# An S5 and gated DeltaNet step on one core: the second supertile's input projection, taken chunk by chunk

## The chip, the core and the metric

The kernel runs on one core of a Trainium2 chip. TensorE (PE in the profile) multiplies matrices into PSUM, VectorE (DVE) and ScalarE (ACT) do elementwise work, GpSimd (POOL) does more of it, and SyncE (SP) issues DMA transfers, as ACT and POOL can too. Each engine works through its own instructions in an order that is fixed when the program is built, and waits for the others on semaphores. The metric is the device time of one execution in microseconds (us); of several runs the median counts.

## What is computed

A two-layer streaming encoder step over 2048 prompt positions and 8 x 16 sample positions, width 1024. Cut to what matters here:

```python
def trunk(x, c, ...):
    cs = jax.nn.silu(c)
    for i in range(DEPTH):                      # layer 0: S5, layer 1: gated DeltaNet
        mod = cs @ w_ada[i] + b_ada[i]
        shift, scale, gate = jnp.split(mod[:, None, :], 3, axis=-1)
        h = rms_norm(x, norm_g[i]) * (1.0 + scale) + shift
        ...                                     # the mixer of the layer, on h
        x = x + gate * out
    y = rms_norm(x, final_g)

def s5_branch(h, ...):
    proj = h @ w_in
    u, z = jnp.split(proj, 2, axis=-1)
    ...                                         # scan over u, gates, output projection
```

The prompt has one row of `c`, so one shift and one scale per channel; each of the eight sample sequences has its own. The change lies in the first lines of layer 0: the norm and modulation of x and the product that gives `u`.

## The kernel before

**Tiling.** Channels lie on the partitions. The 2176 positions are eight supertiles of 272 columns (`NCH`): 256 of the prompt (`NPC`) and 16 of the samples. A supertile's x is a tile of 128 partitions by 8 chunks of channels by 272 columns. Its u has eight blocks of 128 output channels. Each block is one PSUM tile, the sum over the eight chunks. `mm3` (L146) makes a float32 product of three matmuls per chunk: the high part of the weight times the high part of x, high times low, low times high. "High" is a copy in a narrower type (`hh`), "low" (`hl`) is what is left of x after the high part is taken away.

**Norm and modulation.** `norm_sq` (L249) squares x on ACT and adds halves on DVE, `norm_r` (L259) sums over channels with a matmul into the tile `ms` and takes square root and reciprocal, and `norm_mul` (L270) multiplies all eight chunks by it in one DVE instruction. `apply_mod` (L277) then multiplies by the scale and adds the shift, sample columns on DVE for all chunks together, prompt columns on ACT chunk by chunk, makes high and low parts for halves of four chunks, and stores h to memory (L299). For supertile 1 it is called with `first=True`: ACT writes the high part at once, and DVE does the modulation in place a second time, followed by one subtraction per half for the low part.

**Order.** Engine proxies `T`, `V`, `S`, `SY` (L57) can be put in an ordered mode: then each instruction on them is held behind the one written before it. Outside this mode a planner that runs at build time orders each engine's instructions. Supertile 0 (L380 to L412) is ordered, chunk by chunk, while weights arrive. Its PSUM tiles for blocks 2 to 5 come from a pool of four (`psd4`), the others from a pool of two (`psd`). L413 to L425 is the passage of the change: the norm of supertile 1's x (`xt1`), evictions of blocks 0 and 1 (`first_copy`, L373, an ACT copy and a store), the split of the last two weight blocks, `apply_mod` of supertile 1, and then the products of blocks 6 and 7 of supertile 0 and the evictions of blocks 2 to 7. PE's own order has the norm's matmul first and blocks 6 and 7 of supertile 0 behind it. After that the loop at L567 takes supertiles 1 to 7: for each of eight blocks one PSUM tile from `psd4`, 24 matmuls, an eviction (`store_u`, L307). Ahead of the fifth block of each supertile (cb == 4) it modulates the next one and loads the one after it. For j == 0 it does no products; it takes `hnext`, loads x2 and norms it, ordered behind the passage above on DVE and ACT.

**Work beside it.** Operations on small tables fill DVE: `transitions` (L483) and the chains ahead of it may run at any time, `rot_table` (L552) only behind the last ordered DVE instruction of the passage (`after`, L424). The pools `sq`, `acc` and `r` of the norm have one buffer each; x has three, so that x4's load waits for the store of h from supertile 1. `SY` is ordered until L581.

Of the kernel before, what the change touches and what calls it, by code (L numbers as in the profile page):

```python
# [10 lines left out]
F32 = mybir.dt.float32  # L11
F32R = mybir.dt.float32r
I32 = mybir.dt.int32
AF = mybir.ActivationFunctionType
ALU = mybir.AluOpType
# [3 lines left out]
P = 128  # L19
D = 1024  # L20
KC = 8
NTOK = 2176
NCH = 272
NPC = 256
# [17 lines left out]
def bc(ap, axis, n):  # L42
    a = ap.unsqueeze(axis)
    shape = list(a.shape)
    shape[axis] = n
    return a.broadcast_to(shape)
# [7 lines left out]
def kernel(ctx: ExitStack, tc: tile.TileContext, I, O, upto="Z"):  # L54
    nc = tc.nc
# [18 lines left out]
    T, V, S, G, SY = (Engine(e) for e in (nc.tensor, nc.vector, nc.scalar, nc.gpsimd, nc.sync))  # L74
# [10 lines left out]
    h0_d = [dr.tile([D, NCH], F32, name=f"h0_d{i}") for i in range(8)]  # L85
# [23 lines left out]
    modT = cst.tile([P, 48, 9], F32, name="modT")  # L109
    gs0 = cst.tile([P, 8, 9], F32, name="gs0")  # L110
# [35 lines left out]
    def mm3(ps, w_hi, w_lo, x_hi, x_lo, part=None):  # L146
        n = len(w_hi)
        for k in part or range(n):
            T.matmul(ps, lhsT=w_hi[k], rhs=x_hi[k], start=(k == 0), stop=False)  # L149
            T.matmul(ps, lhsT=w_hi[k], rhs=x_lo[k], start=False, stop=False)  # L150
            i_ = T.matmul(ps, lhsT=w_lo[k], rhs=x_hi[k], start=False, stop=(k == n - 1))  # L151
        return i_.ins
# [51 lines left out]
    def pairs(pool, nm):  # L204

        t = {(o, i): pool.tile([P, KC, P], F32R, tag=f"{i}{o}", name=f"{nm}{i}{o}")
             for o in range(7, -1, -1) for i in "hl"}
        return [t[o, "h"] for o in range(8)], [t[o, "l"] for o in range(8)]
# [4 lines left out]
    def ks(t, n=KC):  # L213
        return [t[:, k] for k in range(n)]
# [4 lines left out]
    wu_hi, wu_lo = pairs(wp, "wu")  # L219
    ev = pab.enter_context(tc.tile_pool(reuse_waits="tile", name="ev", bufs=3))  # L220
    xz = pab.enter_context(tc.tile_pool(reuse_waits="tile", name="xz", bufs=1))
    psd = pab.enter_context(tc.tile_pool(reuse_waits="tile", name="psd", bufs=2, space=PSUM))
# [4 lines left out]
    def split_x(nm, xt, hf):  # L227
        a = hp.tile([P, 4, NCH], F32R, tag="hh", name=f"hh{nm}_{hf}")
        b = hp.tile([P, 4, NCH], F32R, tag="hl", name=f"hl{nm}_{hf}")
        spl["i"] = [S.copy(a, xt).ins, V.tensor_sub(b, xt, a.bitcast(F32)).ins]  # L230
        return ks(a, 4), ks(b, 4)

    with ExitStack() as pa:
# [6 lines left out]
        hp = pa.enter_context(tc.tile_pool(reuse_waits="tile", name="hp", bufs=4))  # L240
        psn = pa.enter_context(tc.tile_pool(reuse_waits="tile", name="psn", bufs=1, space=PSUM))
        psd4 = pa.enter_context(tc.tile_pool(reuse_waits="tile", name="psd4", bufs=4, space=PSUM))

        def load_x(j):
            xt = xp.tile([P, KC, NCH], F32, tag="x", name=f"x{j}")
            ld = SY.dma_start(xt, I["xT"][:, j * NCH:(j + 1) * NCH].rearrange("(k p) n -> p k n", p=P))
            return xt, ld.ins

        def norm_sq(xt, sqs=None):  # L249
            acc = sp1.tile([P, 2, NCH], F32, tag="acc", name="acc")  # L250
            for hf in range(2):
                sq = sqs[:, 4 * hf:4 * hf + 4] if sqs else sp1.tile([P, 4, NCH], F32, tag="sq", name="sq")
                xh = xt[:, 4 * hf:4 * hf + 4]
                S.activation(sq, xh, AF.Square)
                V.tensor_add(sq[:, 0:2], sq[:, 0:2], sq[:, 2:4])
                V.tensor_add(acc[:, hf], sq[:, 0], sq[:, 1])
            return acc

        def norm_r(acc, r=None, fold=False):  # L259
            ps = psn.tile([P, NCH], F32, tag="ms", name="ms")  # L260
            if fold:
                V.tensor_add(acc[:, 0], acc[:, 0], acc[:, 1])
            for hf in range(1 if fold else 2):
                T.matmul(ps, lhsT=onesd, rhs=acc[:, hf], start=(hf == 0), stop=(fold or hf == 1))
            r = sp1.tile([P, NCH], F32, tag="r", name="r") if r is None else r
            S.activation(r, ps, AF.Sqrt, bias=epst)
            V.reciprocal(r, r)
            return r

        def norm_mul(xt, r):  # L270
            V.tensor_mul(xt, xt, bc(r, 1, KC))
            return xt

        def norm_x(xt, fold=False):
            return norm_mul(xt, norm_r(norm_sq(xt), fold=fold))

        def apply_mod(j, xt, first=False):  # L277
            xs = xt[:, :, NPC:NCH].rearrange("p k (q h) -> p k q h", h=2)
            V.tensor_mul(xs, xs, bc(gs0[:, :, 1:9], 3, 2))
            V.tensor_add(xs, xs, bc(modT[:, 0:8, 1:9], 3, 2))  # L280
            hl = []
            for hf in range(2):
                k4 = range(4 * hf, 4 * hf + 4)
                if not first:
                    for k in k4:
                        xk = xt[:, k, 0:NPC]
                        S.activation(xk, xk, AF.Identity, scale=gs0[:, k, 0:1], bias=modT[:, k, 0:1])
                    hl.append(split_x(j, xt[:, 4 * hf:4 * hf + 4], hf))
                    continue
                a, b = (hp.tile([P, 4, NCH], F32R, tag=t, name=f"{t}{j}_{hf}") for t in ("hh", "hl"))  # L290
                S.copy(a[:, :, NPC:NCH], xt[:, 4 * hf:4 * hf + 4, NPC:NCH])
                for i, k in enumerate(k4):
                    xk = xt[:, k, 0:NPC]
                    S.activation(a[:, i, 0:NPC], xk, AF.Identity, scale=gs0[:, k, 0:1], bias=modT[:, k, 0:1])
                    V.tensor_scalar(xk, xk, gs0[:, k, 0:1], modT[:, k, 0:1], op0=ALU.mult, op1=ALU.add)
                V.tensor_sub(b, xt[:, 4 * hf:4 * hf + 4], a.bitcast(F32))
                hl.append((ks(a, 4), ks(b, 4)))
            (h0, l0), (h1, l1) = hl
            nc.scalar.dma_start(h0_d[j].rearrange("(k p) n -> p k n", p=P), xt)  # L299
            return h0 + h1, l0 + l1  # L300
# [6 lines left out]
        def store_u(j, cb, ps):  # L307
            o = eva.tile([P, NCH], F32, tag="o", name=f"ev{j}_{cb}")
            S.copy(o, ps)
            nc.scalar.dma_start(u_d[cb][j], o)  # L310
# [7 lines left out]
        pd0 = [(psd if cb < 2 else psd4).tile([P, NCH], F32, tag="d", name=f"pd0_{cb}") for cb in range(6)]  # L318
        h0 = [[hp.tile([P, 4, NCH], F32R, tag=f"h{i}", name=f"h{i}0_{hf}") for hf in range(2)] for i in "hl"]
        hcur = [ks(t[0], 4) + ks(t[1], 4) for t in h0]  # L320
# [52 lines left out]
        def first_copy(cb):  # L373
            store_u(0, cb, pd0[cb])
# [12 lines left out]
        for k in range(KC):  # L387
# [5 lines left out]
            if k == 6:  # L393
                xt1 = load_x(1)[0]
# [18 lines left out]
        acc1 = norm_sq(xt1, xsq)  # L413
        first_copy(0)
        first_copy(1)
        for w in raws:
            split_raw(*w)
        hnext = apply_mod(1, norm_mul(xt1, norm_r(acc1)), True)
        for cb in range(2, 8):
            if cb > 5:  # L420
                pd0 += [psd.tile([P, NCH], F32, tag="d", name=f"pd0_{cb}")]
                mm3(pd0[cb], ks(wu_hi[cb]), ks(wu_lo[cb]), *hcur)
            first_copy(cb)
        after = [V.last]  # L424
        T.ordered = V.ordered = S.ordered = False  # L425
        nc.scalar.dma_start(h0_d[0].rearrange("(k p) n -> p k n", p=P), xcur)
# [140 lines left out]
        for j in range(8):  # L567
            hh, hl = hcur
            T.ordered = j == 1
            for cb in range(8):  # L570
                if cb == 4:
                    if j < 7:
                        hcur = apply_mod(j + 1, xnext) if j else hnext
                    V.ordered = S.ordered = j == 0
                    if j < 6:
                        xn, xl = load_x(j + 2)
                        if j == 0:
                            xnext = norm_x(xn)
                    V.ordered = S.ordered = False
                    s5_tables(j)  # L580
                    SY.ordered = False  # L581
                    with later(after):
                        for i in range(3 * j, min(3 * j + 3, 16)):
                            rot_table(i)
                if j > 0:
                    ps = psd4.tile([P, NCH], F32, tag="d", name=f"pd{j}_{cb}")
                    i_ = mm3(ps, ks(wu_hi[cb]), ks(wu_lo[cb]), hh, hl)
                    store_u(j, cb, ps)
                if cb == 7 and 0 < j < 6:
                    xnext = norm_x(xn)  # L590
                if j > 1 and cb % 3 == 1:
                    with later([xl, i_]):
                        ada.pop(0)()
# [10 lines left out]
    hp = pab.enter_context(tc.tile_pool(reuse_waits="tile", name="hpz", bufs=3))  # L604
# [214 lines left out]
    with ExitStack() as px:  # L819
# [96 lines left out]
        for j in range(8):  # L916
# [56 lines left out]
            for ob in range(8):  # L973
                if ob > 1:
# [3 lines left out]
                                       op0=ALU.mult, op1=ALU.add)  # L978
# [302 lines left out]
    with pd:  # L1281
# [15 lines left out]
        pd1 = pd.enter_context(ExitStack())  # L1297
# [4 lines left out]
        first = [psd1.tile([P, 512], F32, tag="d", name=f"pc0_{n0}") for n0, n in NATT]  # L1302
# [132 lines left out]
        with ExitStack() as pq:  # L1435
# [51 lines left out]
            for i0, (n0, n) in enumerate(NATT):  # L1487
                ps = psd1.tile([P, 512], F32, tag="d", name=f"pba{n0}")[0:32, 0:n]
                hh, hl = hcols(n0, n)
# [284 lines left out]
    if True:  # L1774
# [159 lines left out]
        for t in range(16):  # L1934
            p, nx = pp[t], pp.get(t + 1)
# [151 lines left out]
```

## Time and profile before

| | |
|---|---|
| runs | 2149.6, 2155.93, 2157.43 us (median 2155.93) |
| profiled execution | 2152.21 us, span 2150.5 us |
| busy share of the span | PE 97%, DVE 73%, ACT 45%, POOL 22% |
| granted TensorE clock, mean | 0.980 |
| PE busy, 0 to 59.2 us | 41.15 us |
| PE busy, 99.2 to 140 us | 40.80 of 40.80 us |

A row of the timeline has the start in us from the span's start, the duration in us, the engine, the line, the operation, the tiles (written <- read) with their shapes, and in brackets the idle time before it and what ended it. Buffer numbers are left out of tile names: `pd` is any PSUM tile of the projection, `hl` the low part of any supertile. Instructions that were issued in ordered mode show L69, the proxy's line, in place of their own. Rows that follow closely on one engine overlap, since the engines are pipelined. In rows of stretches, each engine has its busy us and its count, and behind POOL stand the granted clock (1.00 is full), the busy share of the DMA engines and GB/s.

### The profile page before, as it was taken

How to read it: one execution, taken by the hardware profiler on the slowest of the kernel's cores; microseconds unless marked ns; L12 is line 12 of the kernel's file. 1: busy time of each engine (PE TensorE's matmuls, PEld its weight loads, DVE VectorE, ACT ScalarE, POOL GpSimd, SP SyncE). 2: the span in 40 equal slices, each digit the busy share in tenths (PEclk: the TensorE clock that was granted, in tenths of full speed). 3: DMA queues.
4: the chain of work that ended last, by engine and by line, in shares of the span. 5: the costliest groups of instructions: out<-in, count | busy, mean ns of one | idle time of the engine just before them, and what ended most of it. 6: DMA issues, size and time to landing. Idle time of an engine off the chain costs nothing. (4 is left out here: it accounts for less than half of the span.)

```text
span 2150.5 us, 42173 instructions
## 1 busy us (share of the span) xinstructions
PE 2086.0 (97%) x15729; PEld 1853.2 (86%) x15729; DVE 1560.0 (73%) x4017; ACT 973.0 (45%) x2290; POOL 477.7 (22%) x720
## 2 busy tenths in 40 slices
PE   6899999999799999999999999999999899999998
PEld 4888988888599999999888879889987788888887
DVE  6999598999756544446665669688546888888875
ACT  3543433333255444446665422341224556666663
POOL 1267410000112222222100000100011344444430
PEclk7999999999899999999999999999999899999999
DMA  9796854454284333336466213663456644444532
GB/s 279 269 300 226 247 150 143 139 161 149 92 243 151 107 113 110 108 100 218 139 207 181 83 42 86 161 147 101 137 165 208 201 138 134 133 138 147 147 113 69
DMA packets 395209, 332.40 MB, mean 155 GB/s; under 512 B 88026, under 2 KB 358890, under 8 KB 395004
## 3 DMA queue, kind: packets, MB, share of 16 engines
q1 hardware_dynamic: 259084, 226.56, 35.8%
q10 hardware_dynamic: 133104, 95.49, 13.9%
q0 software_dynamic: 2816, 7.65, 1.0%
q8 instruction: 124, 2.03, 0.4%
q14 instruction: 81, 0.66, 0.1%
HBM read 213.01 MB, written 116.61 MB: 153 GB/s over the span
## 5 line engine op out<-in xcount | busy, mean ns | idle before, releaser
L149 PE MATMUL pc<-h1h,wdh 128*128 128x512 f32 (+1 forms) x600 | 216.4, 361 | 0.0
L150 PE MATMUL pc<-h1l,wdh 128*128 128x384 f32 (+1 forms) x600 | 214.8, 358 | 0.3 <-POOL h1l L1340 0.3
L151 PE MATMUL pc<-h1h,wdl 128*128 128x384 f32 (+1 forms) x600 | 214.9, 358 | 0.0
L1400 DVE SCALAR_TENSOR_TENSOR ac<-pb,convw,ac 128x384 f32<-128x384 f32 (+3 forms) x288 | 163.5, 591 | 3.3
L149 PE MATMUL pdz<-hhz,wzh 128*128 128x272 f32 x512 | 151.3, 296 | 2.0 <-ACT evz L626 2.0
L150 PE MATMUL pdz<-hlz,wzh 128*128 128x272 f32 x512 | 152.0, 297 | 0.0
L149 PE MATMUL po<-gh,woh 128*128 128x272 f32 x512 | 148.8, 291 | 2.2 <-ACT gh L933 2.2
L151 PE MATMUL pdz<-hhz,wzl 128*128 128x272 f32 x512 | 150.7, 294 | 0.0
L149 PE MATMUL pg<-yh,wgh 128*128 128x272 f32 x512 | 148.2, 289 | 1.9 <-ACT evz L626 1.9
L150 PE MATMUL pg<-yl,wgh 128*128 128x272 f32 x512 | 149.1, 291 | 0.0
L151 PE MATMUL po<-gh,wol 128*128 128x272 f32 x512 | 148.6, 291 | 0.0
L151 PE MATMUL pg<-yh,wgl 128*128 128x272 f32 x512 | 148.2, 289 | 0.0
L150 PE MATMUL po<-gl,woh 128*128 128x272 f32 x512 | 147.8, 289 | 0.0
L149 PEld LDWEIGHTS pc<-h1h,wdh 128*128 128x128 f32 x600 | 112.6, 188 | 12.3 <-issue 1.7
L150 PEld LDWEIGHTS pc<-h1l,wdh 128*128 128x128 f32 x600 | 112.7, 188 | 10.7 <-issue 0.8
L151 PEld LDWEIGHTS pc<-h1h,wdl 128*128 128x128 f32 x600 | 112.6, 188 | 10.1 <-issue 0.8
L149 PE MATMUL pd<-hh,wuh 128*128 128x272 f32 x384 | 112.5, 294 | 0.0
L69 PE MATMUL epo<-w2h,ohi 128*128 128x512 f32 x272 | 111.5, 410 | 0.0
L151 PE MATMUL pd<-hh,wul 128*128 128x272 f32 x384 | 110.9, 289 | 0.0
L150 PE MATMUL pd<-hl,wuh 128*128 128x272 f32 x384 | 110.6, 288 | 0.0
L69 PE MATMUL epo<-w2h,olo 128*128 128x512 f32 x272 | 106.9, 393 | 0.0
L69 PE MATMUL epo<-w2l,ohi 128*128 128x512 f32 x272 | 106.9, 393 | 0.0
(613 smaller groups left out, 6335.9 us busy)
## 6 DMA issues: line engine op xcount, KB each, us to landing
wa<-in_w_ada SPq DMA_DIRECT2D x32, 512.0 KB
wdr<-in_w_in SPq DMA_DIRECT2D x24, 512.0 KB
h_d<-x ACTq DMA_DIRECT2D x8, 1088.0 KB
u_d<-ev ACTq DMA_DIRECT2D x64, 136.0 KB
hz<-h_d SPq DMA_DIRECT2D x16, 544.0 KB
u<-u_d SPq DMA_DIRECT2D x16, 544.0 KB
z_d<-evz ACTq DMA_DIRECT2D x64, 136.0 KB
y_d<-y ACTq DMA_DIRECT2D x32, 272.0 KB
```

The lines of the kernel that those rows point to most:

```text
L69: i_ = f(*a, **kw)
L149: T.matmul(ps, lhsT=w_hi[k], rhs=x_hi[k], start=(k == 0), stop=False)
L150: T.matmul(ps, lhsT=w_hi[k], rhs=x_lo[k], start=False, stop=False)
L151: i_ = T.matmul(ps, lhsT=w_lo[k], rhs=x_hi[k], start=False, stop=(k == n - 1))
L1400: V.scalar_tensor_tensor(o, src(j), convw[:, b, j:j + 1], o, op0=ALU.mult, op1=ALU.add)
```

## The change

Supertile 1's modulation leaves `apply_mod` and is written out in the passage. The sample columns of all chunks are normed and modulated first. The evictions of blocks 2 to 5 of supertile 0 are put ahead of the modulation, which frees the four tiles of `psd4`; these are taken by blocks 0 to 3 of supertile 1 at once. Then, chunk by chunk, the prompt columns are multiplied by the norm factor, ACT writes the high part, DVE modulates in place and subtracts the low part, and PE multiplies this chunk into all four tiles. The evictions of blocks 6 and 7 come after the second and third chunk, the store of h after the last. In the loop, the first four blocks of supertile 1 have only their evictions left.

```diff
-        def apply_mod(j, xt, first=False):
+        def apply_mod(j, xt):
             xs = xt[:, :, NPC:NCH].rearrange("p k (q h) -> p k q h", h=2)
             V.tensor_mul(xs, xs, bc(gs0[:, :, 1:9], 3, 2))
             V.tensor_add(xs, xs, bc(modT[:, 0:8, 1:9], 3, 2))
             hl = []
             for hf in range(2):
-                k4 = range(4 * hf, 4 * hf + 4)
-                if not first:
-                    for k in k4:
-                        xk = xt[:, k, 0:NPC]
-                        S.activation(xk, xk, AF.Identity, scale=gs0[:, k, 0:1], bias=modT[:, k, 0:1])
-                    hl.append(split_x(j, xt[:, 4 * hf:4 * hf + 4], hf))
-                    continue
-                a, b = (hp.tile([P, 4, NCH], F32R, tag=t, name=f"{t}{j}_{hf}") for t in ("hh", "hl"))
-                S.copy(a[:, :, NPC:NCH], xt[:, 4 * hf:4 * hf + 4, NPC:NCH])
-                for i, k in enumerate(k4):
+                for k in range(4 * hf, 4 * hf + 4):
                     xk = xt[:, k, 0:NPC]
-                    S.activation(a[:, i, 0:NPC], xk, AF.Identity, scale=gs0[:, k, 0:1], bias=modT[:, k, 0:1])
-                    V.tensor_scalar(xk, xk, gs0[:, k, 0:1], modT[:, k, 0:1], op0=ALU.mult, op1=ALU.add)
-                V.tensor_sub(b, xt[:, 4 * hf:4 * hf + 4], a.bitcast(F32))
-                hl.append((ks(a, 4), ks(b, 4)))
+                    S.activation(xk, xk, AF.Identity, scale=gs0[:, k, 0:1], bias=modT[:, k, 0:1])
+                hl.append(split_x(j, xt[:, 4 * hf:4 * hf + 4], hf))
...
         for w in raws:
             split_raw(*w)
-        hnext = apply_mod(1, norm_mul(xt1, norm_r(acc1)), True)
-        for cb in range(2, 8):
-            if cb > 5:
-                pd0 += [psd.tile([P, NCH], F32, tag="d", name=f"pd0_{cb}")]
-                mm3(pd0[cb], ks(wu_hi[cb]), ks(wu_lo[cb]), *hcur)
+
+        r1 = norm_r(acc1)
+        x1s = xt1[:, :, NPC:NCH]
+        V.tensor_mul(x1s, x1s, bc(r1[:, NPC:NCH], 1, KC))
+        x1q = x1s.rearrange("p k (q h) -> p k q h", h=2)
+        V.tensor_mul(x1q, x1q, bc(gs0[:, :, 1:9], 3, 2))
+        V.tensor_add(x1q, x1q, bc(modT[:, 0:8, 1:9], 3, 2))
+        for cb in (6, 7):
+            pd0 += [psd.tile([P, NCH], F32, tag="d", name=f"pd0_{cb}")]
+            mm3(pd0[cb], ks(wu_hi[cb]), ks(wu_lo[cb]), *hcur)
+        for cb in range(2, 6):
             first_copy(cb)
+        pd1 = [psd4.tile([P, NCH], F32, tag="d", name=f"pd1_{cb}") for cb in range(4)]
+        h1 = [[hp.tile([P, 4, NCH], F32R, tag=f"h{i}", name=f"h{i}1_{hf}") for hf in range(2)] for i in "hl"]
+        hnext = [ks(t[0], 4) + ks(t[1], 4) for t in h1]
+        for hf in range(2):
+            S.copy(h1[0][hf][:, :, NPC:NCH], xt1[:, 4 * hf:4 * hf + 4, NPC:NCH])
+            for k in range(4 * hf, 4 * hf + 4):
+                xk, hk = xt1[:, k, 0:NPC], hnext[0][k]
+                V.tensor_mul(xk, xk, r1[:, 0:NPC])
+                S.activation(hk[:, 0:NPC], xk, AF.Identity, scale=gs0[:, k, 0:1], bias=modT[:, k, 0:1])
+                V.tensor_scalar(xk, xk, gs0[:, k, 0:1], modT[:, k, 0:1], op0=ALU.mult, op1=ALU.add)
+                V.tensor_sub(hnext[1][k], xt1[:, k], hk.bitcast(F32))
+                for cb in range(4):
+                    mm3(pd1[cb], ks(wu_hi[cb]), ks(wu_lo[cb]), *hnext, range(k, k + 1))
+                if k in (1, 2):
+                    first_copy(5 + k)
+        nc.scalar.dma_start(h0_d[1].rearrange("(k p) n -> p k n", p=P), xt1)
         after = [V.last]
         T.ordered = V.ordered = S.ordered = False
...
-                if j > 0:
+                if j == 1 and cb < 4:
+                    store_u(1, cb, pd1[cb])
+                elif j > 0:
                     ps = psd4.tile([P, NCH], F32, tag="d", name=f"pd{j}_{cb}")
                     i_ = mm3(ps, ks(wu_hi[cb]), ks(wu_lo[cb]), hh, hl)
                     store_u(j, cb, ps)
```

## The prediction

> **What bounds the kernel now.** I read the page first, then the stretches around the second supertile, then the timelines of TensorE (PE), VectorE (DVE) and ScalarE (ACT) between 49 and 130 us, then PE's waits. The page says that PE is the engine to watch, so a PE gap is worth its length as long as nothing behind it takes it back.
>
> ```profile
> span 2150.5 us, 42173 instructions
> PE 2086.0 (97%) x15729; PEld 1853.2 (86%) x15729; DVE 1560.0 (73%) x4017; ACT 973.0 (45%) x2290; POOL 477.7 (22%) x720
> ```
>
> The stretches show the gap: busy us and instructions of PE, PEld, DVE, ACT, POOL, then the granted clock.
>
> ```profile
> 66.96:72.23 5.27, 0.00 (x1) 0.00 (x1) 5.17 (x26) 4.66 (x12) 0.00 (x0) 0.73 0.86 314
> 72.23:76.20 3.97, 3.97 (x17) 3.97 (x18) 3.97 (x21) 2.36 (x6) 0.00 (x0) 0.50 0.74 255
> 76.20:87.11 10.91, 10.91 (x86) 10.75 (x84) 10.79 (x83) 4.66 (x7) 0.00 (x0) 1.00 0.95 333
> ...
> 128.69:268.80 140.11, 140.11 (x1088) 126.47 (x1085) 109.64 (x521) 55.31 (x98) 86.72 (x224) 1.00 0.80 256
> ```
>
> PE is empty for 5.27 us, then runs at clock 0.50: 17 matmuls in 3.97 us, 0.23 us each, against 0.127 us each in the next row. The pause costs 5.27 + 17 x 0.10 = 7.0 us; that is the most the change can win here. From 128.69 us PE has no hole for 140 us, and DVE is busy in almost all of the three rows above: it is the second engine to watch.
>
> ```profile
> 72.23 0.59 PE L69 MATMUL pd<-hh,wuh 128*128 128x272 f32 x1 [5.27 <-ACT ev L69]
> ...
> 67.57 0.24 ACT L69 CAST hh<-x 128x64 fp32r<-128x64 f32 x1 [5.29 <-DVE x L69]
> 73.47 1.12 ACT L69 ACTIVATE sq<-x 128x1088 f32<-128x1088 f32 x1
> ...
> 64.22 2.42 DVE L69 TENSOR_TENSOR x<-x,r 128x2176 f32<-128x2176 f32 x1
> 66.86 0.28 DVE L69 TENSOR_TENSOR x<-x,gs 128x128 f32<-128x128 f32 x1
> 73.33 1.29 DVE L69 TENSOR_TENSOR hl<-x,hh 128x1088 fp32r<-128x1088 f32 x1
> ```
>
> PE waits for an eviction that ACT does after the whole modulation of x1, and ACT waits 5.29 us for DVE's product over 2176 columns. The second low part is ready at 73.33 + 1.29 = 74.62.
>
> **The first half of supertile 1.** Its 96 matmuls (four blocks, eight chunks, three each) stay 96. The 2.42 us product becomes three sample operations of 128 columns (0.28 us each, with handover about 0.9 in all: 64.22 to 65.1) and eight products of 256 columns; two low parts of 1088 columns become eight of 272. The evictions of blocks 2 to 5 move ahead of the modulation into ACT's 5.29 us of waiting, so they cost nothing; without that cover they would cost PE what they cost now. A chunk is a strict chain, since the in-place modulation on DVE may only write after ACT has read, and DVE's order is written by hand. Supertile 0 has the same chain:
>
> ```profile
> 49.63 0.43 DVE L69 TENSOR_TENSOR x<-x,r 128x272 f32<-128x272 f32 x1
> ...
> 52.27 0.41 DVE L69 TENSOR_SCALAR x<-x,gs,modT 128x256 f32<-128x256 f32 x1
> ...
> 52.78 0.45 DVE L69 TENSOR_TENSOR hl<-x,hh 128x272 fp32r<-128x272 f32 x1
> 53.14 0.42 DVE L69 COPY mA<-ada 128x256 f32<-128x256 f32 x1
> ...
> 51.63 0.60 ACT L69 ACTIVATE hh<-x,modT,gs 128x256 fp32r<-128x256 f32 x1 [3.16 <-DVE gs L69]
> ```
>
> Product 0.43, handover 0.03 (89.51 to 89.54 in the rows of x2 below), ACT's start to DVE's modulation 0.64 (51.63 to 52.27), to the low part 0.51 (52.78), to the next instruction 0.36 (53.14): a step is 1.97 us. PE needs 12 x 0.127 = 1.52 for it, so PE waits 0.45 a step. Chunk 0: 65.1 + 0.43 + 0.03 + 0.64 + 0.51 + 0.45 = 67.16, against PE free at 66.96: the gap shrinks from 5.27 to 0.2. Chunk 7 is ready at 67.16 + 7 x 1.97 = 80.95, and PE is done at 82.5. Before, the same 96 ended at 87.11, with 0.52 of norm sums among them: **PE leads by 4.1 us** there. A step could be 1.7 (no handover between the ends of instructions) or 2.3 (three more small operations between).
>
> **What is late next.** The norm of x2 is ordered by hand behind the last chunk on ACT and DVE, so its first square, at 73.47 now, starts after ACT's chunk 7: 65.56 + 7 x 1.97 + 0.6 = 79.9, **6.4 us later**. Its chain to PE, now:
>
> ```profile
> 75.06 0.72 DVE L69 TENSOR_TENSOR sq<-sq 128x544 f32<-128x544 f32 x1
> 76.30 0.44 DVE L69 TENSOR_TENSOR acc<-sq 128x272 f32<-128x272 f32 x1
> ...
> 82.49 0.62 PE L264 MATMUL ms<-acc,onesd 128*128 128x272 f32 x2
> ...
> 83.15 0.49 ACT L69 ACTIVATE r<-ms,epst 128x272 f32<-128x272 f32 x1 [1.51 <-PE ms L264]
> ...
> 84.24 1.84 DVE L69 RECIPROCAL r<-r 128x272 f32<-128x272 f32 x1
> ...
> 87.09 2.42 DVE L69 TENSOR_TENSOR x<-x,r 128x2176 f32<-128x2176 f32 x1
> ...
> 89.54 0.60 ACT L287 ACTIVATE x<-x,modT,gs 128x256 f32<-128x256 f32 x1 [1.84 <-DVE x L69]
> 92.15 3.54 ACT L287 ACTIVATE x<-x,modT,gs 128x256 f32<-128x256 f32 x7
> 95.86 1.10 ACT L230 CAST hh<-x 128x1088 fp32r<-128x1088 f32 x1
> ...
> 97.86 1.28 DVE L230 TENSOR_TENSOR hl<-x,hh 128x1088 fp32r<-128x1088 f32 x1
> ...
> 99.21 1.08 PE L69 MATMUL ms<-acc,onesd 128*128 128x272 f32 x4
> 99.93 0.87 PE L149 MATMUL pd<-hh,wuh 128*128 128x272 f32 x4
> ```
>
> x2's first low part ends at 99.14 and PE takes it at 99.93: **0.8 us of slack**, the thinnest of the stage. PE will now be there at 82.5 + 12.82 (87.11 to 99.93) + 0.52 (the norm sums that now fall here) = 95.8. The chain takes 25.7 us (73.47 to 99.14). Its own durations are two squares, two pairs of adds (2 x 2.28), 0.62, 0.49, 1.84, 2.42, eight activations (4.1), 1.10, 1.28: 16.4, and 17.0 with a dozen handovers of 0.05. So the low part comes between 79.9 + 17.0 = 96.9 and 79.9 + 25.7 = 105.6. The other 8.7 us are other work in DVE's and ACT's queues: transition and rotation operations, and the squares of later supertiles. One part of it leaves, 34 transition operations, the first and last of which are
>
> ```profile
> 74.68 0.19 DVE L465 TENSOR_TENSOR sm<-gk 128x32 f32<-128x32 f32 x1
> ...
> 94.17 0.18 DVE L505 TENSOR_TENSOR ni<-sm 128x32 f32<-128x32 f32 x1
> ```
>
> at about 0.11 us of queue each, 3.7 us. They fit into DVE's waits in the chunk steps (eight times some 0.9 us: 1.97 less three slots of about 0.35). I take 25.7 - 3.7 = 22.0 us, near the upper end, because DVE's queue was full all this time and the rotation tables, which may start only behind the last chunk, move along with x2. The low part then ends at 101.9 and PE starts supertile 2 at 102.0, **2.1 us later than now**, after a pause of 6.2 us. That is longer than the pause of 5.27, so the slow clock moves here too: 17 x 0.10 = 1.8. Sum: +2.1 + 1.8 = **+3.9 us**. The gain of the first half is spent.
>
> **Behind it.** Supertile 3 has room: its second low part ends at 125.04 and PE starts it at 128.69.
>
> ```profile
> 123.76 1.28 DVE L230 TENSOR_TENSOR hl<-x,hh 128x1088 fp32r<-128x1088 f32 x1
> ...
> 128.69 0.39 PE L149 MATMUL pd<-hh,wuh 128*128 128x272 f32 x1
> ```
>
> If x3 moved by all of 6.4 it would come at 131.4, before the 12 matmuls of its first half are done at 128.7 + 3.9 + 1.5 = 134.1. The store of h moves behind chunk 7 on ACT's queue, and SP's next load waits for that buffer:
>
> ```profile
> 73.61 0.41 ACTq L299 DMA_DIRECT2D h_d<-x  x1
> ...
> 78.94 0.38 SPq L246 DMA_DIRECT2D x<-in_xT  x1
> 79.44 3.22 SPq L180 DMA_DIRECT2D wa<-in_w_ada  x5
> ...
> 107.52 1.07 PE L186 MATMUL ada<-wa,cs 128*32 128x512 f32 x8
> ```
>
> Store to load is 5.3 us. With the store at some 80.5, x4 is issued at 85.8 and the five weight loads queued behind it end their issue at 89.5 instead of 82.7; the first such product is at 107.52, so I cost this at nothing (if they landed after it: up to 7 us more). Evictions of blocks 0 to 3 now fall together after chunk 7, two squares of x2 among them; block 4 needs the first bank 1.1 us after it is complete, so 0 to 0.5 us.
>
> **The time.** The profiled execution took 2152.21 us around its span of 2150.5; +3.9 gives 2156.1. The runs shown, 2149.6 to 2157.43, have their median 3.7 above it. With the profiled one the four average 2153.8, and I add to that: 2157.7, rounded to 2158.
>
> **Rivals.** *The lead is kept.* If x2's chain shrinks to its own durations plus two or so us, its low part comes at 97 to 98.9 and PE starts supertile 2 1 to 2.9 us earlier than now, with a short pause and no slow clock: 2151 to 2153. For it: 8.7 us of the chain is other work, and the norm sum at 82.49 waited 2.2 us for PE (adds of the second half end near 80.2), which runs earlier now. Against: DVE was busy throughout. Chance 0.23.
>
> *x2 stays behind the rotation tables.* DVE's queue then keeps all 25.7 us, or also takes the 4 us of wide table operations that now come after 97.86 us ahead of the low part. (Three tables are 129 operations; 109 of them stand ahead of 97.86, some 20 of this kind behind, at 0.2 us of queue each.)
>
> ```profile
> 99.53 0.28 DVE L451 TENSOR_TENSOR q<-tw,gk 128x128 f32<-128x128 f32 x1
> ```
>
> Every us behind 99.9 counts in full: +5.8 to +9.8, and 1.8 for the clock: 2161 to 2165. It is slower than before, and decides as soon as the low part is ready after 99.9. For it: the low part stood 0.9 us in DVE's queue after its cast was done (95.86 + 1.10 to 97.86). Against: the norm itself comes before the tables in program order. Chance 0.15.
>
> *The clock falls in the chunk loop.* PE would rest 0.45 us in every 1.97. Here is where the trace shows a fall without one long gap:
>
> ```profile
> 1694.85:1697.57 2.72, 0.44 (x16) 0.36 (x16) 2.27 (x5) 2.66 (x12) 1.23 (x1) 0.99 1.04 280
> 1697.58:1704.90 7.32, 6.53 (x88) 5.63 (x88) 5.90 (x13) 3.21 (x16) 3.42 (x2) 0.54 0.05 8
> ```
>
> PE was idle 84% of 2.7 us there; the chunk loop leaves 23% idle, far from it. If it fell all the same, a chunk takes 12 x 0.23 = 2.76 us, the first half ends at 67.2 + 22.1 = 89.3 and supertile 2 starts at 102.6: +2.7, about 2156.5, and the first rival is dead. The Trainium skill, TensorE: Matmul & The Clock Gate, section "A second HAM failure mode: psum-queue depth-cycling", speaks for this case: short idles between groups of matmuls that cycle through PSUM made the clock swing between half and full. By that rule the change would win nothing in its first half; the rows above don't show it for idles this short. Chance 0.05.
>
> *The change doesn't close its gap* (PE still waits for chunk 0, or steps take over 2.3 us): chunk 7 and x2 come 2 to 3 us later still, about 2161. Chance 0.05. A different static order of later stages, better or worse by 10 us or more, has the last 0.04.
>
> **How the numbers follow.** The forecast has 0.48 and by itself spans +1 to +6, 2155 to 2160. The range takes in the first two rivals and the spread of the runs (some 4 us each way): 2148 to 2167. A measurement tells about 0.5% from no change, 10.8 us, which is more than the 7.0 us at stake: within it 0.89; faster needs a better order elsewhere, 0.04; slower needs the second rival's upper end or a worse order, 0.07.
>
> **What would show it.** Right: no 5.27 us gap at 67; eight groups of 12 matmuls some 2 us apart, each waiting for DVE's low part; x2's first square near 80; a PE pause of several us before supertile 2 near 96, released by DVE's L230, with clock 0.50 behind it. Wrong: steps of 1.5 us or over 2.3, a low part of x2 before 98, a pause elsewhere (an eviction before block 4, a weight load near 107), or stages behind 300 us that differ by more than the shift.

## The result and the profile after

The changed kernel takes 2169.05 us (median of 5 runs, 2166.7 to 2173.48), the kernel before 2155.12 us beside it (5 runs, 2149.6 to 2157.43). The ratio is 1.0073, 95% interval 1.0059 to 1.0087: **slower by 0.7%, some 14 us**, where 2158 was forecast and the range ended at 2167. The pause that the change was aimed at became shorter, and another one, twice as long, appeared 30 us later.

The first two lines of the page of the changed kernel:

```profile
span 2166.4 us, 42187 instructions
PE 2093.2 (97%) x15729; PEld 1855.3 (86%) x15729; DVE 1566.2 (72%) x4031; ACT 973.8 (45%) x2290; POOL 488.4 (23%) x720
```

Stretches of it (columns as before: PE, PEld, DVE, ACT, POOL, granted clock, DMA share, GB/s), from the end of supertile 0's products on:

```profile
66.60:68.86 2.26, 0.00 (x1) 0.01 (x1) 0.02 (x1) 0.75 (x2) 0.00 (x0) 1.00 1.08 389
68.86:84.74 15.88, 13.90 (x94) 12.17 (x94) 15.40 (x75) 6.46 (x13) 2.45 (x6) 1.00 0.34 128
...
98.72:111.04 12.32, 3.22 (x9) 1.75 (x9) 12.32 (x41) 8.97 (x14) 10.39 (x26) 0.65 0.68 252
111.04:115.97 4.93, 4.93 (x22) 4.93 (x23) 4.93 (x19) 1.68 (x4) 2.86 (x4) 0.50 0.58 166
...
140.00:280.00 140.00, 140.00 (x1083) 125.52 (x1083) 102.02 (x477) 56.06 (x99) 80.86 (x186) 1.00 0.76 242
```

Row 1 is what is left of the old pause: 2.26 us instead of 5.27. Row 2 is the chunk loop at full clock. Row 3 is the new pause: of 12.32 us PE is busy 3.22, with norm sums and a few first products, and in row 4 it pays with half the clock for the 22 matmuls behind it. From 140 us PE has no hole again. For 4.50 us of the pause PE stands at a norm sum of x4, which its order has ahead of supertile 2; x2's high part is ready only at 105.78, so this wait decides nothing. Here is who ends the new pause (timeline of PE), and what the ending instruction waited for (timelines of DVE and ACT, changed kernel):

```profile
104.62 1.24 PE L264 MATMUL ms<-acc,onesd 128*128 128x272 f32 x2 [4.50 <-DVE acc L256]
105.84 1.27 PE L149 MATMUL pd<-hh,wuh 128*128 128x272 f32 x4
111.04 0.59 PE L150 MATMUL pd<-hl,wuh 128*128 128x272 f32 x1 [3.93 <-DVE hl L230]
```

```profile
92.84 1.84 DVE L69 RECIPROCAL r<-r 128x272 f32<-128x272 f32 x1
...
95.96 2.51 DVE L69 TENSOR_TENSOR x<-x,r 128x2176 f32<-128x2176 f32 x1
...
102.24 1.84 DVE L267 RECIPROCAL r<-r 128x272 f32<-128x272 f32 x1
...
105.70 2.44 DVE L271 TENSOR_TENSOR x<-x,r 128x2176 f32<-128x2176 f32 x1
108.06 0.47 DVE L697 TENSOR_TENSOR ca<-sp 128x288 f32<-128x288 f32 x1
108.75 0.45 DVE L697 TENSOR_TENSOR ca<-sp 128x288 f32<-128x288 f32 x1
109.61 1.37 DVE L230 TENSOR_TENSOR hl<-x,hh 128x1088 fp32r<-128x1088 f32 x1
...
82.48 1.10 ACT L69 ACTIVATE sq<-x 128x1088 f32<-128x1088 f32 x1
...
104.70 1.08 ACT L230 CAST hh<-x 128x1088 fp32r<-128x1088 f32 x1
```

x2's first square starts at 82.48 (73.47 before), and its low part ends at 110.98 (99.14 before). The chain has not only moved, it is 28.5 us long instead of 25.7. Between x2's product (95.96) and x2's low part (109.61) DVE runs the whole reciprocal and product of x3 (L267, L271) and table work of the next stage (`ca`). x2's high part is ready at 105.78, and the low part still waits 3.8 us in DVE's queue. In the kernel before, x2's low part stands at 97.86, ahead of x3's reciprocal and product, which have almost the same times as now:

```profile
102.03 1.85 DVE L267 RECIPROCAL r<-r 128x272 f32<-128x272 f32 x1
...
105.45 2.42 DVE L271 TENSOR_TENSOR x<-x,r 128x2176 f32<-128x2176 f32 x1
```

Where the 15.9 us between the two spans (2150.5 and 2166.4) arise can be read from the same matmul in both: the first one of the z projection, and the first `sp<-sr` product of the last stage. The first pair of rows is before and after, the second pair likewise.

```profile
268.82 0.37 PE L149 MATMUL pdz<-hhz,wzh 128*128 128x272 f32 x1
```

```profile
281.13 0.37 PE L149 MATMUL pdz<-hhz,wzh 128*128 128x272 f32 x1
```

```profile
1605.75 0.49 PE L1237 MATMUL sp<-sr,xf 128*128 128x128 f32 x2
```

```profile
1617.00 0.49 PE L1250 MATMUL sp<-sr,xf 128*128 128x128 f32 x2
```

12.3 us are lost by the z projection, 11.3 by the last stage. Each is a difference of two single executions; experiment 8 shows how far one kernel's can lie apart. The last stage takes 544.7 us in the one profile and 549.4 in the other, though its instructions stand in the same order; the eighth experiment shows that this part is chance.

### The profile page after: what moved, and what is told of

It reads as the page before. It is cut to its first block, busy times and chain, and to the rows that moved or that the text cites. A ratio compares the mean times of both kernels' runs of the same rounds, so it can differ in the third digit from the quotient of the medians.

```text
span 2166.4 us, 42187 instructions
## 1 busy us (share of the span) xinstructions
PE 2093.2 (97%) x15729; PEld 1855.3 (86%) x15729; DVE 1566.2 (72%) x4031; ACT 973.8 (45%) x2290; POOL 488.4 (23%) x720
```

## The experiments

All are the changed kernel with one thing altered, if nothing else is said. Times are medians; the ratio is to runs of the kernel before on the same chip.

### 1. x2's norm no longer ordered

```diff
-                    V.ordered = S.ordered = j == 0
                     if j < 6:
                         xn, xl = load_x(j + 2)
```

> The changed kernel, with one thing taken back: the norm of x2 is not held behind the last chunk on VectorE and ScalarE, the planner may put it into the waits of the chunk loop. Theory A (x2's norm starts too late, and that is the loss): its first square runs well before 82 us, its low part is ready by 95 to 100 us instead of 111, the pause before supertile 2 shrinks from 12 us to 0 to 3, and the kernel takes 2152 to 2158 us. Theory B (VectorE's queue is full up to 110 us whatever the order): the low part stays at 107 to 111 us and the kernel within 3 us of the changed one, 2166 to 2172.

Measured: 2156.58 us (2155.07 to 2160.71), ratio 1.0019 (1.0008 to 1.0031), against 1.0073: about three quarters of the loss are gone. PE no longer pauses before supertile 2. The squares of x2 now run inside the loop:

```profile
67.36 1.11 ACT L254 ACTIVATE sq<-x 128x1088 f32<-128x1088 f32 x1 [4.54 <-DMA sp<-in_cN]
70.09 1.11 ACT L254 ACTIVATE sq<-x 128x1088 f32<-128x1088 f32 x1 [0.97 <-DVE acc L256]
```

```profile
98.10 1.28 DVE L230 TENSOR_TENSOR hl<-x,hh 128x1088 fp32r<-128x1088 f32 x1
```

The first low part of x2 (second fence, DVE) ends at 99.38, as Theory A expected. In this stage the loop pays for it, and supertile 2 starts at 102.88 instead of 99.93: the clock is 0.50 from 71.36 to 74.78, and the planner put other work between the chunks, on DVE x2's reciprocal ahead of the last low part, which slipped to 88.14 (83.06 in the changed kernel). By 1605 us this profile is level with the kernel before (its last stage begins at 1605.41, there at 1605.75). Theory B falls: DVE's queue is not so full that the order wouldn't matter.

### 2. Stores of the early evictions from GpSimd's queue

```diff
-            nc.scalar.dma_start(u_d[cb][j], o)
+            (E or nc.scalar).dma_start(u_d[cb][j], o)
...
         for cb in range(2, 6):
-            first_copy(cb)
+            first_copy(cb, nc.gpsimd)
```

> The changed kernel, with the stores of the four early evictions (blocks 2 to 5 of supertile 0) issued from GpSimd's queue in place of ScalarE's. In the changed kernel ScalarE stands 5 us between them, behind small table loads, and chunk 0 starts 2.6 us later than forecast. If those store issues are what holds ScalarE: the first chunk's high part starts near 65.5 us in place of 68.2, the loop and x2 come 2.6 us earlier, and the kernel takes 2 to 4 us less than the changed one, 2165 to 2167. Rival: ScalarE waits for something else (VectorE's sample columns), and nothing moves.

Measured: 2165.3 us (2163.44 to 2168.17), ratio 1.0055 (1.0036 to 1.0074). The two intervals overlap, but the trace shows the mechanism. ScalarE in the changed kernel, and then here:

```profile
62.64 5.38 ACTq L299 DMA_DIRECT2D u_d<-ev  x3
68.06 0.24 ACT L69 CAST hh<-x 128x64 fp32r<-128x64 f32 x1 [5.00 <-DMA sp<-in_cN]
68.21 0.60 ACT L69 ACTIVATE hh<-x,modT,gs 128x256 fp32r<-128x256 f32 x1
```

```profile
62.28 1.24 ACT L69 COPY ev<-pd 128x272 f32<-128x272 f32 x4
65.54 0.25 ACT L69 CAST hh<-x 128x64 fp32r<-128x64 f32 x1 [2.02 <-DVE x L69]
65.88 0.60 ACT L69 ACTIVATE hh<-x,modT,gs 128x256 fp32r<-128x256 f32 x1
```

Three store issues take 5.38 us there: ScalarE holds at semaphores ahead of the third and the fourth. By the semaphore events in the trace, each store first waits for the completion semaphore that it will use itself, until the transfer that had it before has landed. For the third that is a load of x issued by SP (landed at 66.06, store issued at 66.13), for the fourth SP's load of small tables (67.28 and 67.68). With the stores elsewhere ScalarE waits for VectorE's sample columns only, and chunk 0 starts 2.3 us earlier (65.88 for 68.21), the low part of x2 2.3 us as well (107.33 for 109.61).

### 3 and 5. x3's norm, or the first tables, held behind x2's low part

```diff
                 if cb == 7 and 0 < j < 6:
-                    xnext = norm_x(xn)
+                    with later(spl["i"] if j == 1 else ()):
+                        xnext = norm_x(xn)
```

> The changed kernel, with the norm of x3 held behind the low part of x2 on VectorE and ScalarE. In the changed kernel x3's reciprocal (1.8 us), product (2.4 us) and its adds stand in VectorE's queue ahead of x2's low part. If they are a part of the loss: the low part comes 4 to 7 us earlier (104 to 107 us), and the kernel takes 2162 to 2165 us. If the planner only fills the place with table operations: no change, 2167 to 2171.

Measured: 2166.88 us (2164.22 to 2167.86), ratio 1.0059 (1.0040 to 1.0078). This is nearer to the second forecast: x2's low part is only 2.2 us earlier, behind table operations. DVE:

```profile
107.46 1.30 DVE L230 TENSOR_TENSOR hl<-x,hh 128x1088 fp32r<-128x1088 f32 x1
```

```diff
+                    if j == 1:
+                        after = spl["i"]
                     with later(after):
-                        for i in range(3 * j, min(3 * j + 3, 16)):
+                        for i in range(0 if j == 1 else 3 * j, min(3 * j + 3, 16) if j else 0):
                             rot_table(i)
```

> The changed kernel, with the first rotation tables held on VectorE behind the low part of x2 (in the changed kernel: behind the last chunk of x1). Theory A2 (x2 starts late, and the table operations in VectorE's queue then stretch its chain from 17 to 28 us): the first square stays at 82.5 us, the low part comes at 101 to 105 us instead of 111, the kernel takes 2158 to 2164 us. Theory A1 (only the late start counts, the table operations just fill holes): the low part stays within 2 us of 111 and the kernel at 2166 to 2171.

Measured: 2168.82 us (2168.6 to 2171.45), ratio 1.0068 (1.0053 to 1.0084). Theory A2 falls as it was put, and Theory A1's numbers come out: taking the tables away alone gains nothing. DVE of the kernel with the tables held:

```profile
103.84 1.85 DVE L267 RECIPROCAL r<-r 128x272 f32<-128x272 f32 x1 [2.82 <-ACT r L266]
105.61 0.76 DVE L699 TENSOR_TENSOR ca<-sp 128x288 f32<-128x288 f32 x2
106.92 0.82 DVE L699 TENSOR_TENSOR ca<-sp 128x288 f32<-128x288 f32 x2
107.66 2.42 DVE L271 TENSOR_TENSOR x<-x,r 128x2176 f32<-128x2176 f32 x1
110.00 2.49 DVE L230 TENSOR_TENSOR hl<-x,hh 128x1088 fp32r<-128x1088 f32 x2
```

DVE even stands idle 2.82 us for x3's square root. x2's high part is there by 105.85, when PE uses it, but the low part stands behind `ca` and x3's product until 110.00: a fixed order doesn't let the ready instruction pass. With x3 held instead, rotation tables and `ca` stood there. Each filled the place that the other left. ScalarE took a part too: without the tables x2's product was ready at 95.67 (98.47 in the changed kernel), but a store held ScalarE until 98.12.

### 9. Both held

The two edits of 3 and 5 together.

> The changed kernel, with both the first tables and the norm of x3 held behind the low part of x2; loop and stores as in the changed kernel. Held alone, neither helped much: the planner put the other one into the place. Theory A3 (x2's chain is stretched by whatever the planner finds for VectorE and ScalarE, so both must go): the first square stays at 82, the low part ends at 101 to 104 us instead of 111, and the kernel takes 2159 to 2163 us. Theory A1 (only the late start counts): low part within 2 us of 111, kernel 2167 to 2171.

Measured: 2160.88 us (2159.42 to 2164.29), ratio 1.0025 (1.0014 to 1.0036). Theory A3 holds by the time; the first low part ends at 104.7, a little behind the expected span. Timelines of DVE and PE:

```profile
92.44 2.43 DVE L69 TENSOR_TENSOR x<-x,r 128x2176 f32<-128x2176 f32 x1
103.43 2.49 DVE L230 TENSOR_TENSOR hl<-x,hh 128x1088 fp32r<-128x1088 f32 x2 [7.63 <-ACT hh L230]
```

```profile
103.45 1.28 PE L149 MATMUL pd<-hh,wuh 128*128 128x272 f32 x4 [5.90 <-ACT hh L230]
```

The chain is 23.0 us now (first square 81.75, first low part to 104.7), and DVE idles at its end: ScalarE is last. It has its own obstacle, the same as in experiment 2:

```profile
97.72 0.33 ACTq L299 DMA_DIRECT2D u_d<-ev  x1
98.09 4.04 ACT L285 ACTIVATE x<-x,modT,gs 128x256 f32<-128x256 f32 x8 [3.14 <-DMA wa<-in_w_ada]
```

The product of x2 is ready at 94.87 and ScalarE begins at 98.09, since a store of u ahead of it (issued at 97.72) was held until a weight load had landed (97.64). That load had used the store's completion semaphore before.

### 4. The early evictions alone

The kernel before, with products 6 and 7 and evictions 2 to 5 ahead of the old `apply_mod`:

```diff
-        hnext = apply_mod(1, norm_mul(xt1, norm_r(acc1)), True)
-        for cb in range(2, 8):
-            if cb > 5:
-                pd0 += [psd.tile([P, NCH], F32, tag="d", name=f"pd0_{cb}")]
-                mm3(pd0[cb], ks(wu_hi[cb]), ks(wu_lo[cb]), *hcur)
-            first_copy(cb)
+        r1 = norm_r(acc1)
+        for cb in (6, 7):
+            pd0 += [psd.tile([P, NCH], F32, tag="d", name=f"pd0_{cb}")]
+            mm3(pd0[cb], ks(wu_hi[cb]), ks(wu_lo[cb]), *hcur)
+        for cb in range(2, 6):
+            first_copy(cb)
+        hnext = apply_mod(1, norm_mul(xt1, r1), True)
+        for cb in (6, 7):
+            first_copy(cb)
```

> The kernel before, with only this part of the change: blocks 6 and 7 of supertile 0 and the evictions of blocks 2 to 5 are put ahead of the modulation of x1; no chunk loop, the norm of x2 as before. If the chunk loop is what moves x2 and so causes the loss, this costs nothing: 2152 to 2158 us, supertile 1 starts within 1 us of 72.2, since its low part is ready only then. Rival: the early evictions with their stores on ScalarE's queue are what hurts: 3 us or more slower than before, with ScalarE held between the stores.

Measured: 2155.82 us (2151.89 to 2159.33), ratio 1.0001 (0.9987 to 1.0015). This part by itself costs and wins nothing; the loss needs the chunk loop. ScalarE, here:

```profile
61.73 5.41 ACTq L310 DMA_DIRECT2D u_d<-ev  x3
67.18 0.24 ACT L69 CAST hh<-x 128x64 fp32r<-128x64 f32 x1 [5.09 <-DVE gk L479]
```

The stores hold ScalarE as long as in the changed kernel, but here the hold is covered: in the kernel before, ScalarE waits for VectorE until 67.57 anyway. With the loop VectorE is ready earlier (ScalarE starts at 65.54 in experiment 2), and the stores are what is left.

### 6. The norm product one chunk ahead

```diff
+        norm_k(0)
...
-                V.tensor_mul(xk, xk, r1[:, 0:NPC])
                 S.activation(hk[:, 0:NPC], xk, AF.Identity, scale=gs0[:, k, 0:1], bias=modT[:, k, 0:1])
+                if k < 7:
+                    norm_k(k + 1)          # V.tensor_mul of chunk k+1 by r1
```

> The changed kernel, with the norm product of chunk k+1 on VectorE moved ahead of the in-place modulation of chunk k, so that ScalarE needn't wait for it. If the step of 1.94 us is the chain product, high part, modulation, low part: VectorE's step falls below PE's 1.52 us, ScalarE's chunk 7 and x2's first square come 5 to 6 us earlier (77 us), and as x2's chain follows the kernel takes 2161 to 2165 us. If the step is set by the load of VectorE and not by the chain: step stays at 1.8 to 1.95, kernel 2167 to 2171.

Measured: 2159.96 us (2154.29 to 2171.59), ratio 1.0023 (1.0006 to 1.0040), a little below the expected span. The first and the last low part of the loop, here and then in the changed kernel:

```profile
68.98 0.43 DVE L69 TENSOR_TENSOR hl<-x,hh 128x272 fp32r<-128x272 f32 x1
...
77.98 0.43 DVE L69 TENSOR_TENSOR hl<-x,hh 128x272 fp32r<-128x272 f32 x1
```

```profile
69.37 0.43 DVE L69 TENSOR_TENSOR hl<-x,hh 128x272 fp32r<-128x272 f32 x1
...
83.06 0.50 DVE L69 TENSOR_TENSOR hl<-x,hh 128x272 fp32r<-128x272 f32 x1
```

Seven steps in 9.0 us, 1.29 each, where the changed kernel needs 1.96. So the step was the chain through two engines, not DVE's load. x2's first square follows at 76.98, 5.5 us earlier, and PE takes the second matmul of supertile 2 at 105.32 in place of 111.04.

### 10 and 7. Loop and stores; loop, stores and both holds

> The changed kernel, with the norm product one chunk ahead and the stores of the early evictions on GpSimd's queue, and nothing held behind x2. If the gains add: x2's first square near 74.5 us, its low part ends 2 to 3 us before the 105.3 us that the norm product ahead alone gave, PE starts supertile 2 at 101 to 103.5, and the kernel takes 2155 to 2159 us, so that holding the tables and x3 back is worth some 5 us on top of it.

Measured: 2158.49 us (2152.83 to 2164.24), ratio 1.0011 (0.9999 to 1.0024). First square 75.21, first low part to 102.96, as expected.

> All together: stores of the early evictions from GpSimd's queue, norm product one chunk ahead, tables and the norm of x3 behind the low part of x2. If the loss is x2's late and stretched chain and the changed kernel's loop itself is good: PE goes from 67 us to supertile 2 with a pause of 0 to 3 us there, starts it near 95 us (99.9 before, 111 in the changed kernel), and the kernel takes 2147 to 2152 us, 3 to 7 less than before. If something else bounds the stage (VectorE's total load), it stays at 2155 or more.

Measured: 2151.3 us (2148.77 to 2154.78), ratio 0.9978 (0.9969 to 0.9988), faster than before. Timeline of PE:

```profile
94.99 0.76 PE L149 MATMUL pd<-hh,wuh 128*128 128x272 f32 x4 [2.40 <-ACT hh L230]
96.31 0.59 PE L150 MATMUL pd<-hl,wuh 128*128 128x272 f32 x1 [0.57 <-DVE hl L230]
```

The holds are worth the step from 1.0011 to 0.9978 here, some 7 us, where the expectation said some 5.

### 11. x2's squares in the loop, by hand

The four edits, and x2's square and adds behind the chunks of index 4 and 6:

```diff
+        def square2(hf):
+            sq = sp1.tile([P, 4, NCH], F32, tag="sq", name="sq2")
+            S.activation(sq, x2[:, 4 * hf:4 * hf + 4], AF.Square)
+            V.tensor_add(sq[:, 0:2], sq[:, 0:2], sq[:, 2:4])
+            V.tensor_add(acc2[:, hf], sq[:, 0], sq[:, 1])
...
                 if k in (1, 2):
                     first_copy(5 + k)
+                if k in (4, 6):
+                    square2(k // 2 - 2)
...
-                            xnext = norm_x(xn)
+                            xnext = norm_mul(x2, norm_r(acc2))
```

> The version with all four edits, and x2's two squares and their adds put into the chunk loop by hand, behind the chunks of index 4 and 6. If the rest of the pause before supertile 2 (2.4 us) is x2's start behind the last chunk: its norm sum comes some 2.5 us earlier, the pause falls to 0 to 1 us, and the kernel takes 2148 to 2152 us, 0 to 2.5 less than with the four edits. Rival: the adds delay chunks 5 to 7 on VectorE and PE waits for them instead: no gain, 2150 to 2154.

Measured: **2145.5 us** (2142.69 to 2148.4), ratio **0.9947** (0.9934 to 0.9961), below the expected span and the fastest of all. Stretches of it, and PE's first products of supertile 2:

```profile
66.60:67.04 0.44, 0.01 (x2) 0.00 (x1) 0.44 (x3) 0.10 (x1) 0.00 (x0) 1.00 0.99 366
67.04:79.40 12.36, 12.36 (x95) 12.20 (x96) 11.95 (x55) 6.42 (x12) 0.00 (x0) 1.00 0.56 213
79.40:93.00 13.60, 13.60 (x110) 13.60 (x110) 9.96 (x26) 9.51 (x19) 4.53 (x12) 1.00 0.96 336
```

```profile
92.09 0.54 PE L149 MATMUL pd<-hh,wuh 128*128 128x272 f32 x3
```

The old pause is 0.44 us, the clock stays at 1.00, and PE goes into supertile 2 at 92.09 without a hole. That is 7.8 us ahead of the kernel before (99.93), about the 7.0 us that the prediction put at stake. At the start of the last stage the profile leads by 8.7 us (1597.09 for 1605.75). The medians differ by 11; where the rest arises was not found.

### 8. The kernel before, once more

> The kernel before once more, for its profile: from 1660 us to the end its profiled execution took 490.5 us, while the changed kernel and four variants took 494.7 to 495.9, with the same order of instructions on VectorE, ScalarE and GpSimd. If the last stage differs by chance from execution to execution: about 493 to 496 us here. If the change causes the difference: 490 to 491.

Measured: one run, 2164.5 us, span 2162.8. Its last stage begins here:

```profile
1613.38 0.49 PE L1237 MATMUL sp<-sr,xf 128*128 128x128 f32 x2
```

2162.8 - 1613.4 = 549.4 us, the value of the changed kernel, from the code of the kernel before (counted from 1660 us of the first profile, 7.6 later here, it is 495.2). The other value occurs with the change too: 545.5, 545.1 and 543.4 us in the profiles of experiments 6, 9 and 10. So the 4.7 us in the last stage are chance and no part of the change. This execution is the slowest of the kernel before, and by the z projection it had lost 7.7 us to the first profile. PE waits 2.02 us for a low part until 129.98, 1.01 us for an eviction until 151.98 and 3.44 us for VectorE's `modT` until 197.89, where the first profile has no pause; why wasn't settled.

## Why the prediction was wrong

The mechanism was the forecast one: the gap of supertile 1 moves to supertile 2, because x2's norm is ordered behind the last chunk. The sum was +3.9 us; the stage shows +12.3. Its terms, one by one.

- **"The evictions ... move ahead ... so they cost nothing": failed, 2.6 us.** The copies do fit into ScalarE's wait. The four stores that go with them were counted as free, and two of them hold ScalarE's queue until a load from another queue has landed. Chunk 0's high part starts at 68.21 against some 65.6 forecast, and x2's first square at 82.48 against 79.9: the whole delay of the loop. The old pause therefore shrank to 2.26 us and not to 0.2. Experiment 2 took the stores away and got 2.3 us back.
- **The step of a chunk: right.** 1.97 us forecast, (83.06 - 69.37) / 7 = 1.96 measured; experiment 6 shows that it is the chain that was named.
- **"I take 25.7 - 3.7 = 22.0 us" for x2's chain: failed, 6.5 us.** It is 28.5 us, above the forecast's upper bound of 25.7 too. I had counted what leaves DVE's queue (the transition operations, which did move into the loop) and not what comes in. Up to the high part the chain takes 23.3 us (82.48 to 105.78), where it took 23.5 (73.47 to 96.96): the 3.7 us did not come off. The low part then waits 3.8 us instead of 0.9. x3's norm product did not move: it is at 105.70, where the kernel before has it at 105.45. x2 moved onto it. Before, x3's reciprocal and product came behind x2's low part. Experiment 9, with x3 and the tables out of the way, has 23.0 us.
- **The slow clock behind the pause: right, a little small.** 4.93 us at 0.50, 22 matmuls at 0.10 us each, 2.2 us of cost where 1.8 was forecast.
- **What lies behind: right.** With 2.6, 6.5 and 0.4 for the clock the sum is 3.9 + 9.5 = 13.4. PE did four products of supertile 2 within the pause, which took it 0.7 us before (99.93 to 100.64), and that leaves 12.7, against 12.3 measured at the z projection. The shift stays 11 to 12 us up to the last stage. No late weight load added to it.

Of the rivals, *x2 stays behind the rotation tables* had the right sign and place, 2161 to 2165 for its time, and room for a chain of up to 29.7 us. Its mechanism was too narrow: experiments 3 and 5 show that tables or x3 alone can be taken out with little effect, 9 that both together matter. *The lead is kept* came true only in experiments 7 and 11, where x2's chain was shortened by hand. *The clock falls in the chunk loop* did not happen: the loop rested 12% of its time (13.90 busy of 15.88) and kept 1.00. The Trainium skill (TensorE: Matmul & The Clock Gate, "A second HAM failure mode: psum-queue depth-cycling") tells of short idles between groups of matmuls that made the clock swing. The trace doesn't show it for idles as short as in this loop.

The chances put 0.07 on slower by over 0.5%, and the range ended at 2167. Both came from pricing one delay at a time; the two that failed add up.

## What to carry to other kernels

When work is spread into a loop by an order written by hand, look at what is ordered behind that loop, and give it its slots inside (experiment 11), since that next chain, not the loop, sets when the gain arrives. A chain that is moved in a fixed queue meets other work at its new place: list what stands there, and if two things can fill a place, hold both. Count the stores behind an eviction as instructions of the engine that issues them; moved ahead of a critical step they can cost more than the copies, since each may wait for an older transfer that had its semaphore.

## What was not expected of the hardware

- A store issue can hold its engine's queue for a load of another queue: three issues took 5.38 us on ScalarE in the changed kernel, ended by a load that SP had issued, and one store in experiment 9 held it 3.14 us for a weight load. The trace tells why: the transfers that SP and ACT issue share a few completion semaphores, and an issue waits until the earlier transfer on its semaphore has landed. In experiment 2 the stores on GpSimd's queue have semaphores of their own, and ScalarE does not wait.
- The last stage has two durations with the same order of instructions: 544.7 us in one execution of the kernel before and 549.4 in another. It was 549.4 in the changed kernel and 545.1 in experiment 9.
- Rests of 12% in the chunk loop left the clock at 1.00, and the pause of 12.3 us, a quarter of it busy, brought 0.50 that lasted 4.93 us beyond its end.
